# Two streams of the weights in place of three for experts with up to 64 tokens, chosen by a branch on TensorE

## The chip, the cores and the metric

The kernel runs on one core of a Trainium2 chip. The metric is the time of one execution on the device, in microseconds. A core has TensorE (PE in the profile; its weight loads are PEld), VectorE (DVE), ScalarE (ACT), GpSimd (POOL) and SyncE (SP), each with its own stream of instructions. They meet through semaphores. The DMA engines move data between HBM and the on-chip memory (SBUF); matmuls write into accumulator banks (PSUM).

## The reference

A decoder trunk of two layers over 256 tokens of width 1024, in float32. Each layer has an attention mixer and a feed-forward part; the second layer's feed-forward part is a mixture of eight experts, of which each token uses the two with the largest router logits:

```python
def swiglu(h, w_gate, w_up, w_down):
    return (jax.nn.silu(h @ w_gate) * (h @ w_up)) @ w_down
...
logits = (hf @ router_w).astype(jnp.float32)
top_logit, top_e = lax.top_k(logits, TOP_K)
gate = jax.nn.softmax(top_logit, axis=-1)
...
# every token goes through its two experts; their outputs, weighted by gate, are added
```

w_gate and w_up are 1024 x 3584 for each expert, w_down is 3584 x 1024: 44 MB of weights per expert, 352 MB in all, each read once.

## The kernel before

**Precision.** The matmuls take fp32r operands, which hold fewer bits than fp32. So every fp32 operand is split into an exact sum of two fp32r parts, hi and lo, and a product is three matmuls: x_hi w_hi, x_lo w_hi, x_hi w_lo (`product3`, L364, the matmuls L366 to L368). The weights stream through the three as the moving operand (128 x 512 columns); the tokens are the stationary operand of 128 x 128.

**Weights.** `Weights` (L53) has a list of pieces of 1 MB, 2048 columns on 128 partitions. `load` (L64) issues the DMA of a piece on SP's queue (L71) into a buffer named raw; for the experts there are 4 + 8 such buffers. `take` (L80) makes the two parts of a piece in two halves of 1024 columns: ACT copies raw to fp32r (whi, L94), DVE subtracts that from raw (wlo, L95). There are five buffers of each part (N_PART). A buffer pair is free again when the last matmul that reads it is done, and a raw buffer when both halves are split.

**Experts.** `moe` handles one expert after another. `gather` (L819) picks the expert's tokens into 128 slots (xe, two parts, by matmuls with a one-hot matrix `so`); a slot holds one token, unused slots are zero. An expert with more than 128 tokens is handled by `beyond`, behind a branch at the end (L974); no expert of this input has so many. The 3584 hidden columns are done in seven chunks of 512. For each chunk:

- gate: eg = x w_gate, 8 blocks of 128 rows, 24 matmuls; ACT makes esg = silu (L906);
- up: eu = x w_up, 24 matmuls; DVE makes ehc = eu * esg (L908);
- turn: four transposes of ehc (eT, L914); ACT and DVE split them into eth (L301) and etl (L302);
- down: ey += h w_down, 4 blocks by 2 column halves, 24 matmuls; the bank pair ey is kept over the seven chunks.

Each of the three takes two pieces of weights, four halves, so a chunk has 12 splits on ACT and 12 on DVE, and loads 6 MB.

**Order.** The program is written gate(n), turn(n-1), up(n), down(n-1) (`gate_up`, with `between`). The instructions are placed on each engine by a scheduler that knows which tiles each of them reads and writes, so turn and down may stand elsewhere. Behind an expert's last chunk come `weigh` (yhl, the outputs times their gates, split) and four `scatter` steps, which add the rows back to the tokens (acc, L890); `place` (L855) makes the matrix for it in the chunk with c == 1, and `gather` of the next expert stands at c == 3.

## Time and profile before

| | |
|---|---|
| median of three runs | 1553.09 us (1552.73 to 1553.78) |
| the profiled execution, from first to last instruction | 1555.6 us |
| PE busy | 1527.9 us, 98% |
| DVE busy | 1235.4 us, 79% |
| ACT busy | 1026.8 us, 66% |
| POOL busy | 7.8 us, 17 instructions |
| DMA | 436.94 MB, 281 GB/s over the span |
| mean granted clock of TensorE | 0.993 of full speed |

The profile's times run from the first to the last instruction of one execution; the runs are timed apart from it, with 2.5 us less at the median. "Busy" of PE counts a matmul from its start to its modelled end, and matmuls overlap, so PE is better read by the distance between starts. The part of the time that matters here is the experts' stage, from about 535 to 1548 us. Averages over the whole span mix it with attention and the dense layer.

### The profile page before, as it was taken

Reading aid. Unit: us, or ns where it says so; the run is one execution under the profiler, and the core shown is the slowest. Engines: PE = TensorE matmul, PEld = TensorE weight load, DVE = VectorE, ACT = ScalarE, POOL = GpSimd, SP = SyncE. Lnnn points to the kernel's source line nnn. Section 1 sums busy time; section 2 is a strip of 40 time slices with the busy share of each in tenths; the row PEclk is TensorE's granted clock in tenths of the full one; section 3 lists DMA queues with packets and bytes.
Section 4 is the critical chain, followed back from the end, with each engine's and each line's share of the span. In section 5 each row is a group of like instructions: output and inputs, shape, how many; then the busy total and the mean of one; then the engine's idle time right before and its main releaser. Section 6 shows DMA issues by size and latency. Waiting matters only on the chain.

```text
span 1555.6 us, 20636 instructions
## 1 busy us (share of the span) xinstructions
PE 1527.9 (98%) x7502; PEld 1234.2 (79%) x7502; DVE 1235.4 (79%) x1771; ACT 1026.8 (66%) x1389; POOL 7.8 (1%) x17
## 2 busy tenths in 40 slices
PE   7999999999999999999999999999999999999997
PEld 6767888888777888888888878887887887887885
DVE  5567755555766798998998888988888889888886
ACT  5445644445545587887787777767777776767774
POOL 2000000000000000000000000000000000000000
PEclk9999999999999999999999999999999999999999
DMA  8812455557626499999999989999999999999980
GB/s 263 292 55 82 157 178 177 200 189 234 229 96 217 167 357 331 379 357 329 361 363 333 363 320 336 344 356 342 326 370 352 327 358 346 329 352 365 353 323 29
DMA packets 200907, 436.94 MB, mean 281 GB/s; under 512 B 9448, under 2 KB 26080, under 8 KB 200800
## 3 DMA queue, kind: packets, MB, share of 16 engines
q1 hardware_dynamic: 198160, 434.63, 79.2%
q8 instruction: 61, 1.00, 0.3%
q10 hardware_dynamic: 2176, 0.52, 0.2%
q0 software_dynamic: 464, 0.40, 0.1%
q14 instruction: 46, 0.38, 0.1%
HBM read 433.92 MB, written 1.08 MB: 280 GB/s over the span
## 4 chain that ended last, share of the span: by engine, by line
PE 95%; DMA 2%; DVE 2%; ACT 1%; issue 1%; SPq 0%; ACTq 0%; DVEq 0%
PE eu L368 7%; PE eg L368 7%; PE eu L367 6%; PE eu L366 6%; PE eg L367 6%; PE eg L366 6%; PE ey L366 6%; PE ey L367 6%; PE ey L368 6%; PE pj L368 3%; PE pj L366 3%; PE pj L367 3%; PE y L368 2%; PE y L367 2%; PE y L366 2%; PE o L502 2%
## 5 line engine op out<-in xcount | busy, mean ns | idle before, releaser
L95 DVE TENSOR_TENSOR wlo<-raw,whi 128x1024 fp32r<-128x1024 f32 (+1 forms) x802 | 946.1, 1215 | 158.9 <-ACT whi L94 147.9
L94 ACT ACTIVATE whi<-raw 128x1024 fp32r<-128x1024 f32 (+1 forms) x802 | 807.0, 1051 | 188.7 <-PE y L367 45.2
L368 PE MATMUL eg<-wlo,xe 128*128 128x512 f32 x448 | 177.4, 396 | 1.5 <-DVE wlo L95 1.5
L368 PE MATMUL eu<-wlo,xe 128*128 128x512 f32 x448 | 178.6, 399 | 0.0
L366 PE MATMUL ey<-whi,eth 128*128 128x512 f32 x448 | 177.5, 397 | 0.7 <-ACT eth L301 0.7
L366 PE MATMUL eg<-whi,xe 128*128 128x512 f32 x448 | 176.8, 395 | 0.7 <-ACT xe L304 0.3
L366 PE MATMUL eu<-whi,xe 128*128 128x512 f32 x448 | 177.4, 396 | 0.0
L367 PE MATMUL ey<-whi,etl 128*128 128x512 f32 x448 | 176.8, 395 | 0.0
L367 PE MATMUL eg<-whi,xe 128*128 128x512 f32 x448 | 175.9, 393 | 0.0
L367 PE MATMUL eu<-whi,xe 128*128 128x512 f32 x448 | 175.2, 391 | 0.0
L368 PE MATMUL ey<-wlo,eth 128*128 128x512 f32 x448 | 165.7, 399 | 0.0
L368 PEld LDWEIGHTS eu<-wlo,xe 128*128 128x128 f32 x448 | 84.1, 188 | 23.9 <-DVE wlo L95 6.9
L368 PEld LDWEIGHTS eg<-wlo,xe 128*128 128x128 f32 x448 | 84.2, 188 | 22.4 <-DVE wlo L95 4.6
L366 PEld LDWEIGHTS ey<-whi,eth 128*128 128x128 f32 x448 | 84.3, 188 | 20.7 <-ACT eth L301 1.1
L367 PEld LDWEIGHTS ey<-whi,etl 128*128 128x128 f32 x448 | 84.5, 189 | 20.2 <-DVE etl L302 0.4
L366 PEld LDWEIGHTS eg<-whi,xe 128*128 128x128 f32 x448 | 84.2, 188 | 20.3 <-ACT whi L94 2.6
L367 PEld LDWEIGHTS eg<-whi,xe 128*128 128x128 f32 x448 | 84.1, 188 | 17.8
L367 PEld LDWEIGHTS eu<-whi,xe 128*128 128x128 f32 x448 | 84.2, 188 | 17.1
L366 PEld LDWEIGHTS eu<-whi,xe 128*128 128x128 f32 x448 | 84.2, 188 | 15.8
L368 PEld LDWEIGHTS ey<-wlo,eth 128*128 128x128 f32 x448 | 82.5, 188 | 17.4
L301 ACT ACTIVATE eth<-eT 128x512 fp32r<-128x512 f32 x56 | 33.1, 592 | 88.7 <-PE ey L368 75.0
L366 PE MATMUL pj<-whi,uhi 128*128 128x512 f32 (+1 forms) x192 | 76.3, 399 | 0.8 <-ACT qv L411 0.8
(299 smaller groups left out, 1970.5 us busy)
## 6 DMA issues: line engine op xcount, KB each, us to landing
raw<-in_exp_w_gate_dram SPq DMA_DIRECT2D x112, 1024.0 KB, 7.0
raw<-in_exp_w_up_dram SPq DMA_DIRECT2D x112, 1024.0 KB, 7.0
raw<-in_exp_w_down_dram SPq DMA_DIRECT2D x112, 1024.0 KB, 6.8
raw<-in_w_in_dram SPq DMA_DIRECT2D x20, 1024.0 KB, 6.0
raw<-in_ffn_w_gate_dram SPq DMA_DIRECT2D x10, 1024.0 KB, 5.1
raw<-in_ffn_w_up_dram SPq DMA_DIRECT2D x10, 1024.0 KB, 5.2
raw<-in_ffn_w_down_dram SPq DMA_DIRECT2D x10, 1024.0 KB, 5.1
raw<-in_cmp_w_dram SPq DMA_DIRECT2D x8, 1024.0 KB, 6.2
```

Of the source, the lines that this page charges most:

```text
L94: self.nc.scalar.activation(hi[:, :m * w], src, AF.Copy)
L95: self.nc.vector.tensor_tensor(out=lo[:, :m * w], in0=src, in1=hi[:, :m * w].bitcast(F32), op=ALU.subtract)
L301: act.activation(hi, src, AF.Copy)
L366: pe.matmul(dst, xh, wh, start=first, stop=False)
L367: pe.matmul(dst, xl, wh, start=False, stop=False)
L368: pe.matmul(dst, xh, wl, start=False, stop=last)
L502: pe.matmul(o[:, hd * HD:(hd + 1) * HD], pt[:, c:c + 128], vpj[:, j, vc:vc + HD], start=(j == 0), stop=(j == nj - 1))
```

## The change

The experts' product is made in one of two ways. The number of an expert's tokens is read into a register on PE (`pe.value_load`), and `by_number` puts the matmuls of up, turn and down each into an If with an Else; the condition is number > 64. With more than 64 tokens, the matmuls are those of before. With up to 64, the tokens stand twice in the 128 slots (`own`): slots 0 to 63 and again 64 to 127. `mixed` makes, on POOL, a stationary operand with the hi parts in columns 0 to 63 and the lo parts in columns 64 to 127 (xm for up, htm for down). Then two matmuls per block do the work of three: xm w_hi and xm w_lo, so 16 in up and 16 in down, and the sums of the two slots of a token are added later: in turn by a matrix of two identities (`both`) in place of the transpose, at the end by the scatter. Gate stays as it was. `halves`, `ahead` and `take_half` split the weights ahead of their use, one half at a time, in list order, since a split can't stand inside an arm of a branch.

The diff, cut to its core (the other changed lines are comments, blank lines, and lines moved from further down):

```diff
-    def take(self):
-        """The two parts of the next piece, for each of its blocks of 128 rows."""
+    def halves(self):
         while self.used in self.plain:
             self.used += 1
         raw = self.take_raw(self.used)
         _, nk, w = self.specs[self.used]
         self.used += 1
-        out = []
...
-            out += [(hi[:, i * w:(i + 1) * w], lo[:, i * w:(i + 1) * w]) for i in range(m)]
-        return out
+            yield [(hi[:, i * w:(i + 1) * w], lo[:, i * w:(i + 1) * w]) for i in range(m)]
+
+    def take(self):
+        return [x for half in self.halves() for x in half]
+
+    def ahead(self, n, loads):
+
+        while n:
+            if self.open is None:
+                if self.used >= len(self.specs):
+                    return
+                self.open = self.halves()
+            half = next(self.open, None)
+            if half is None:
+                self.open = None
+                self.load(self.used + loads)
+            else:
+                self.ready.append(half)
+                n -= 1
+
+    def take_half(self):
+        return self.ready.pop(0)
...
+        few = mpool.tile([128, NE], F32, name="few")
+        dve.tensor_scalar(out=few, in0=cb[:, 0:NE], scalar1=64.0, scalar2=None, op0=ALU.is_le)
+        number = mpool.tile([128, NE], I32, name="number")
+        dve.tensor_copy(number, cb[:, 0:NE])
...
+        again = mpool.tile([128, 128], F32, name="again")
+        dve.memset(again[:, 0:64], 0.0)
+        dve.memset(again[:, 64:128], -64.0)
+        both = mpool.tile([128, 128], F32, name="both")
+        for i in range(2):
+            dve.tensor_tensor(out=both[:, i * 64:(i + 1) * 64], in0=ident[:, 0:64], in1=ident[:, 64:128], op=ALU.add)
...
+            own = mpool.tile([128, 128], F32, name="own", tag="own")
+            dve.scalar_tensor_tensor(out=own, in0=again, scalar=few[:, e:e + 1], in1=slot, op0=ALU.mult, op1=ALU.add)
             so = mpool.tile([128, NT, 128], F32, name="so", tag="so", bufs=2)
             for t in range(NT):
-                dve.tensor_scalar(out=so[:, t, :], in0=slot, scalar1=pos[:, t, e:e + 1], scalar2=None,
+                dve.tensor_scalar(out=so[:, t, :], in0=own, scalar1=pos[:, t, e:e + 1], scalar2=None,
...
-            held[e] = so, x, rl
+            held[e] = so, x, rl, pe.value_load(number[0:1, e:e + 1], min_val=0, max_val=S)
...
-        def gate_up(e, c, between):
...
-            hc = mpool.tile([128, 512], F32, name="ehc", tag="ehc", bufs=2)
+        def by_number(e, many, few):
+
+            with tc.If(held[e][3] > 64) as cond:
+                many()
+            with cond.Else():
+                few()
+
+        def mixed(src, name, n):
+
+            dst = mpool.tile([128, n, 128], F32R, name=name)
+            pool.tensor_copy(dst.rearrange("p k (i t) -> p i k t", i=2), src[:, :, :, 0:64])
+            return dst
+
+        def gate(e):
+            _, x, rl, _ = held[e]
+            b = mm_bank("eg")
+            for half in range(4):
+                for k, (wh, wl) in enumerate(ws.take_half(), half * 2):
+                    product3(b, x[:, 0, k, :], x[:, 1, k, :], wh, wl, k == 0, k == KD - 1)
+                ws.ahead(1, deep)
+            sg = mpool.tile([128, 512], F32, name="esg", tag="esg")
+            act.activation(sg, b, AF.Silu, scale=rl)
+            return sg
+
+        def up(e, sg):
+            _, x, rl, _ = held[e]
+            b = mm_bank("eu")
+            xm = state["xm"]
+            w = [x for _ in range(4) for x in ws.take_half()]
+
+            def many():
+                for k, (wh, wl) in enumerate(w):
+                    product3(b, x[:, 0, k, :], x[:, 1, k, :], wh, wl, k == 0, k == KD - 1)
+
+            def few():
+                for k, (wh, wl) in enumerate(w):
+                    pe.matmul(b, xm[:, k, :], wh, start=(k == 0), stop=False)
+                    pe.matmul(b, xm[:, k, :], wl, start=False, stop=(k == KD - 1))
+
+            by_number(e, many, few)
+            hc = mpool.tile([128, 512], F32, name="ehc", tag="ehc")
             dve.scalar_tensor_tensor(out=hc, in0=b, scalar=rl, in1=sg, op0=ALU.mult, op1=ALU.mult)
             return hc
 
-        def turn(hc):
+        def turn(e, hc):
             b = tr_bank("eT")
-            for f in range(4):
-                pe.transpose(b[:, f * 128:(f + 1) * 128], hc[:, f * 128:(f + 1) * 128], ident)
-            th = mpool.tile([128, 4, 128], F32R, name="eth", tag="eth")
-            tl = mpool.tile([128, 4, 128], F32R, name="etl", tag="etl")
-            split_psum(th.rearrange("p f t -> p (f t)"), tl.rearrange("p f t -> p (f t)"), b)
-            return th, tl
-
-        def down(e, c, th, tl):
+
+            def many():
+                for f in range(4):
+                    pe.transpose(b[:, f * 128:(f + 1) * 128], hc[:, f * 128:(f + 1) * 128], ident)
+
+            def few():
+                for f in range(4):
+                    pe.matmul(b[:, f * 128:(f + 1) * 128], hc[:, f * 128:(f + 1) * 128], both, start=True, stop=True)
+
+            by_number(e, many, few)
+            ht = mpool.tile([128, 2, 4, 128], F32R, name="eth", tag="eth")
+            split_psum(ht[:, 0].rearrange("p f t -> p (f t)"), ht[:, 1].rearrange("p f t -> p (f t)"), b)
+            return ht, mixed(ht, "htm", 4)
+
+        def down(e, c, ht):
             if c == 0:
                 state["y"] = [acc_bank("ey") for _ in range(2)]
             y = state["y"]
             final = c == len(MOE_CHUNKS) - 1
-            w = []
-            for half in range(2):
-                w += ws.take()
-                ks = range(4) if half else ()
-                if not final:
-                    ks = range(half * 2, half * 2 + 2)
-                for k, n in [(k, n) for n in range(2) for k in ks] if final else [(k, n) for k in ks for n in range(2)]:
+            w = [x for _ in range(4) for x in ws.take_half()]
+            ht, htm = ht
+            steps = [(k, n) for n in range(2) for k in range(4)] if final else [(k, n) for k in range(4) for n in range(2)]
+
+            def many():
+                for k, n in steps:
                     f = slice(n * 512, (n + 1) * 512)
-                    product3(y[n], th[:, k, :], tl[:, k, :], w[k][0][:, f], w[k][1][:, f],
+                    product3(y[n], ht[:, 0, k, :], ht[:, 1, k, :], w[k][0][:, f], w[k][1][:, f],
                              c == 0 and k == 0, final and k == 3)
+
+            def few():
+                for k, n in steps:
+                    f = slice(n * 512, (n + 1) * 512)
+                    pe.matmul(y[n], htm[:, k, :], w[k][0][:, f], start=(c == 0 and k == 0), stop=False)
+                    pe.matmul(y[n], htm[:, k, :], w[k][1][:, f], start=False, stop=(final and k == 3))
+
+            by_number(e, many, few)
...
-        parts_of = []
-
-        def between():
-            if prev is not None:
-                parts_of[:] = turn(prev[2])
-
+        deep = N_RAW + SPARE
+        ws.ahead(N_PART, deep)
         for i, (e, c) in enumerate(seq):
             if c == 3 and e + 1 < NE:
                 gather(e + 1)
-            hc = gate_up(e, c, between)
+            if c == 0:
+                state["xm"] = mixed(held[e][1], "xm", KD)
+            sg = gate(e)
+            ht = None
             if prev is not None:
-                down(*prev[:2], *parts_of)
+                ht = turn(prev[0], prev[2])
+            hc = up(e, sg)
+            ws.ahead(4, deep)
+            if prev is not None:
+                down(*prev[:2], ht)
+                ws.ahead(4, deep)
             for _ in range(PER if c else 0):
                 if left:
                     scatter(*left.pop(0))
             prev = (e, c, hc)
-        between()
-        down(*prev[:2], *parts_of)
+        down(*prev[:2], turn(prev[0], prev[2]))
```

The change moves instructions on every engine. Names carry a number for each use of a buffer. On PE, in a chunk of a later expert, the stretch from the end of up to the turn stood like this before: eu is the up product of this chunk, ey are the two halves of the down product of the chunk ahead of it, ehc_10095 is what DVE makes from eu_10050.

```order
L367 MATMUL ey_9439<-whi_10099,etl_10045 128x512
L366 MATMUL ey_9440<-whi_10099,eth_10044 128x512
L367 MATMUL ey_9440<-whi_10099,etl_10045 128x512
L368 MATMUL ey_9439<-wlo_10100,eth_10044 128x512 [waits DVE_49]
L368 MATMUL ey_9440<-wlo_10100,eth_10044 128x512
L366 MATMUL ey_9439<-whi_10103,eth_10044 128x512 [waits Activation_49]
L367 MATMUL ey_9439<-whi_10103,etl_10045 128x512
L366 MATMUL ey_9440<-whi_10103,eth_10044 128x512
L367 MATMUL ey_9440<-whi_10103,etl_10045 128x512
L914 MATMUL eT_10186<-cc_70,ehc_10095 128x128 [waits DVE_49]
L914 MATMUL eT_10186<-cc_70,ehc_10095 128x128 x3
L368 MATMUL ey_9439<-wlo_10104,eth_10044 128x512 [waits DVE_49]
```

Ten matmuls of down stand there between the last of up and the turn; the row behind the turn goes on with down.

On PE after the change, from the last matmuls of up's second arm: eu_8880 is this chunk's up product, ehc_8922 is made from it, eg_9007 is the next chunk's gate product, L978 and L982 are the two arms of the turn, and ey_7928 begins down.

```order
L386 MATMUL eg_9007<-whi_8940,xe_8200 128x512 [waits Activation_49]
L931 COMPARE_AND_BRANCH
L978 MATMUL eT_9054<-cc_70,ehc_8922 128x128 [waits DVE_49,PE_49]
L978 MATMUL eT_9054<-cc_70,ehc_8922 128x128 x3
L931 UNCONDITIONAL_BRANCH
L982 MATMUL eT_9054<-both_4756,ehc_8922 128x128 [waits DVE_49,PE_49]
L982 MATMUL eT_9054<-both_4756,ehc_8922 128x128 x3
L931 UNCONDITIONAL_BRANCH
L387 MATMUL eg_9007<-whi_8940,xe_8200 128x512
L931 COMPARE_AND_BRANCH
L386 MATMUL ey_7928<-whi_8859,eth_8875 128x512
```

One gate matmul now stands between up and the turn, and one between the turn and down, which is now a block of its own.

On PE, the end of that down block (second arm) and what follows:

```order
L1008 MATMUL ey_7928<-wlo_8935,htm_8878 128x512 [waits DVE_49]
L1007 MATMUL ey_7929<-whi_8934,htm_8878 128x512
L1008 MATMUL ey_7929<-wlo_8935,htm_8878 128x512
L931 UNCONDITIONAL_BRANCH
L388 MATMUL eg_9007<-wlo_8941,xe_8200 128x512 [waits DVE_49]
L386 MATMUL eg_9007<-whi_8940,xe_8200 128x512
L387 MATMUL eg_9007<-whi_8940,xe_8200 128x512
L388 MATMUL eg_9007<-wlo_8941,xe_8200 128x512
L386 MATMUL eg_9007<-whi_8985,xe_8200 128x512 [waits Activation_49]
```

Gate goes on with its first buffer pair (whi_8940) only behind the whole down block.

On ACT before, the splits that stand beside up's end and down in the same chunk (whi_10099 to whi_10125 are down's four halves, whi_10144 and whi_10148 the next gate's):

```order
L94 ACTIVATE whi_10099<-raw_10097 128x1024 [waits DMAHW5_49,DVE_49]
L94 ACTIVATE whi_10103<-raw_10097 128x1024 [waits DVE_49,PE_49]
L94 ACTIVATE whi_10121<-raw_10119 128x1024 [waits DMAHW6_49,DVE_49,PE_49]
L94 ACTIVATE whi_10125<-raw_10119 128x1024 [waits DVE_49,PE_49]
L94 ACTIVATE whi_10144<-raw_10142 128x1024 [waits DMAHW7_49,DVE_49,PE_49]
L94 ACTIVATE whi_10148<-raw_10142 128x1024 [waits DVE_49,PE_49]
L301 ACTIVATE eth_10191<-eT_10186 128x512 [waits PE_49]
L94 ACTIVATE whi_10166<-raw_10164 128x1024 [waits DMAHW0_49,DVE_49]
```

They follow each other, and each waits for the matmuls that free its buffer pair, within up or down.

On ACT after (whi_8934 is down's last half, whi_8940, whi_8985, whi_8991 and whi_8995 the next gate's four, whi_9001 and whi_9014 the first two of the next up):

```order
L94 ACTIVATE whi_8934<-raw_8560 128x1024 [waits DVE_49,PE_49]
L94 ACTIVATE whi_8940<-raw_8611 128x1024 [waits DMAHW1_49,DVE_49,PE_49]
L931 UNCONDITIONAL_BRANCH x2
L94 ACTIVATE whi_8985<-raw_8611 128x1024 [waits DVE_49,PE_49]
L94 ACTIVATE whi_8991<-raw_8621 128x1024 [waits DMAHW2_49,DVE_49,PE_49]
L94 ACTIVATE whi_8995<-raw_8621 128x1024
L94 ACTIVATE whi_9001<-raw_8648 128x1024 [waits DMAHW3_49]
L94 ACTIVATE whi_9014<-raw_8648 128x1024 [waits DVE_49,PE_49]
```

whi_8985 waits for a count of PE within the down block, whi_8991 for one that the gate matmuls behind that block reach; the rows after it stand behind it in ACT's queue.

## Rows read from the trace of the kernel before

**Rows 1.** Page, part 4: the chain that ended last, by engine, by line.

```profile
PE 95%; DMA 2%; DVE 2%; ACT 1%; issue 1%; SPq 0%; ACTq 0%; DVEq 0%
PE eu L368 7%; PE eg L368 7%; PE eu L367 6%; PE eu L366 6%; PE eg L367 6%; PE eg L366 6%; PE ey L366 6%; PE ey L367 6%; PE ey L368 6%; PE pj L368 3%; PE pj L366 3%; PE pj L367 3%; PE y L368 2%; PE y L367 2%; PE y L366 2%; PE o L502 2%
```

**Rows 2.** Windows: start:end, length, busy of PE, PEld, DVE, ACT, POOL, clock, DMA share, GB/s.

```profile
600.00:1500.00 900.00, 898.03 (x4113) 730.00 (x4112) 806.70 (x811) 673.62 (x769) 0.00 (x0) 1.00 0.97 349
640.00:660.00 20.00, 20.00 (x93) 16.43 (x92) 18.38 (x18) 16.12 (x18) 0.00 (x0) 1.00 1.03 387
```

**Rows 3.** Chain of waits in pieces, four places: start, us, what.

```profile
918.03 4.80 DMA raw<-in_exp_w_down_dram
...
1008.79 0.23 PE eu L367
...
1011.58 0.44 PE eT L914 x4
...
1045.40 4.76 DMA raw<-in_exp_w_down_dram
```

**Rows 4.** Timeline of SP's queue, two loads of gate weights: start, us, engine, line.

```profile
1380.76 3.91 SPq L71 DMA_DIRECT2D raw<-in_exp_w_gate_dram  x2
...
1397.86 3.91 SPq L71 DMA_DIRECT2D raw<-in_exp_w_gate_dram  x2
```

**Rows 5.** Waits of SP's queue, 840 to 1540 us: total us, times, longest.

```profile
SPq L71 <- DVE wlo L95: 552.4, 216, 5.3
```

**Rows 6.** Lines, 840 to 1540 us, shapes apart: busy us, mean ns, idle before.

```profile
L95 DVE TENSOR_TENSOR wlo<-raw,whi 128x1024 fp32r<-128x1024 f32 x465 | 542.8, 1219 | 37.0 <-ACT whi L94 34.9
L94 ACT ACTIVATE whi<-raw 128x1024 fp32r<-128x1024 f32 x465 | 455.6, 1052 | 12.5 <-PE ey L367 6.0 <-PE eg L367 4.4 <-PE eu L367 1.7
...
L908 DVE SCALAR_TENSOR_TENSOR ehc<-eu,rl,esg 128x512 f32<-128x512 f32 x39 | 29.3, 750 | 18.0 <-PE eu L368 18.0
L302 DVE TENSOR_TENSOR etl<-eT,eth 128x512 fp32r<-128x512 f32 x40 | 27.5, 688 | 10.3 <-ACT eth L301 10.3
...
L890 DVE TENSOR_TENSOR acc<-acc,scat 128x512 f32<-128x512 f32 x22 | 15.0, 683 | 3.1 <-PE scat L889 3.1
...
L305 DVE SCALAR_TENSOR_TENSOR xe<-ga,gv,xe 128x128 fp32r<-128x128 f32 x34 | 10.7, 344 | 1.0 <-ACT xe L304 1.0
...
L305 DVE SCALAR_TENSOR_TENSOR yhl<-ey,gs,yhl 128x512 fp32r<-128x512 f32 x10 | 7.0, 746 | 5.0 <-ACT yhl L304 5.0
```

**Rows 7.** Timeline, all engines, 1002 to 1013 us: start, us, what.

```profile
1008.40 0.39 PE L366 MATMUL eu<-whi,xe 128*128 128x512 f32 x1
...
1008.62 0.39 PE L367 MATMUL eu<-whi,xe 128*128 128x512 f32 x1
...
1009.95 3.48 DVE L95 TENSOR_TENSOR wlo<-raw,whi 128x1024 fp32r<-128x1024 f32 x3
```

**Rows 8.** Windows, early in the program, columns as in rows 2.

```profile
48.76:52.17 3.41, 1.72 (x10) 0.97 (x9) 3.41 (x18) 0.53 (x1) 0.00 (x0) 1.00 1.10 348
52.17:55.58 3.41, 3.41 (x35) 2.09 (x33) 3.27 (x15) 0.00 (x0) 0.00 (x0) 0.50 0.73 193
```

**Rows 9.** Timeline of PE in the second of these: start, us, what.

```profile
52.31 0.63 PE L368 MATMUL pj<-wlo,uhi 128*128 128x512 f32 x1
52.74 0.63 PE L366 MATMUL pj<-whi,uhi 128*128 128x512 f32 x1
```

**Rows 10.** Line L974, the branch before the program's end, by engine: duration in ns.

```profile
L974 ACTq COMPARE_BRANCH  x1: 54/54/54, 1545.6 to 1545.6; - x1
...
L974 PEldq COMPARE_BRANCH  x1: 4622/4622/4622, 1548.2 to 1548.2; - x1
L974 DVEq COMPARE_BRANCH  x1: 72/72/72, 1549.0 to 1549.0; - x1
```

**Rows 11.** Page, part 3: the queue of instructions: packets, MB, share.

```profile
q8 instruction: 61, 1.00, 0.3%
```

More of the change, by code (lines that the diff above doesn't have):

```diff
@@ L816, in moe @@
                                  op0=ALU.add, op1=ALU.mult)
+        cb = tr_bank("count")
+        for t in range(NT):
+            pe.matmul(cb[:, 0:NE], ones, sel[:, t, :], start=(t == 0), stop=(t == NT - 1))
+        few = mpool.tile([128, NE], F32, name="few")
+        dve.tensor_scalar(out=few, in0=cb[:, 0:NE], scalar1=64.0, scalar2=None, op0=ALU.is_le)
+        number = mpool.tile([128, NE], I32, name="number")
+        dve.tensor_copy(number, cb[:, 0:NE])
+        most = mpool.tile([128, 1], F32, name="most")
+        dve.tensor_reduce(out=most, in_=cb[:, 0:NE], axis=AX.X, op=ALU.max)
+        again = mpool.tile([128, 128], F32, name="again")
[4 more added lines that the diff above has]
+            dve.tensor_tensor(out=both[:, i * 64:(i + 1) * 64], in0=ident[:, 0:64], in1=ident[:, 64:128], op=ALU.add)
         rs = row_rstd(h, D, "h")
         def gather(e):
+            own = mpool.tile([128, 128], F32, name="own", tag="own")
+            dve.scalar_tensor_tensor(out=own, in0=again, scalar=few[:, e:e + 1], in1=slot, op0=ALU.mult, op1=ALU.add)
             so = mpool.tile([128, NT, 128], F32, name="so", tag="so", bufs=2)
             for t in range(NT):
-                dve.tensor_scalar(out=so[:, t, :], in0=slot, scalar1=pos[:, t, e:e + 1], scalar2=None,
+                dve.tensor_scalar(out=so[:, t, :], in0=own, scalar1=pos[:, t, e:e + 1], scalar2=None,
                                   op0=ALU.is_equal)
@@ L867, in place @@
             return st, gs
-        cb = tr_bank("count")
-        for t in range(NT):
-            pe.matmul(cb[:, 0:NE], ones, sel[:, t, :], start=(t == 0), stop=(t == NT - 1))
-        most = mpool.tile([128, 1], F32, name="most")
-        dve.tensor_reduce(out=most, in_=cb[:, 0:NE], axis=AX.X, op=ALU.max)
         flag = mpool.tile([128, 1], I32, name="flag")
@@ L893, in moe @@
         state = {}
-        def gate_up(e, c, between):
-            _, x, rl = held[e]
-            for w in range(2):
-                b = mm_bank("eg" if w == 0 else "eu")
-                for half in range(2):
-                    for k, (wh, wl) in enumerate(ws.take(), half * 4):
-                        product3(b, x[:, 0, k, :], x[:, 1, k, :], wh, wl, k == 0, k == KD - 1)
-                    if (w, half) == (0, 1):
-                        between()
-                if w == 0:
-                    sg = mpool.tile([128, 512], F32, name="esg", tag="esg")
-                    act.activation(sg, b, AF.Silu, scale=rl)
-            hc = mpool.tile([128, 512], F32, name="ehc", tag="ehc", bufs=2)
+        def by_number(e, many, few):
[3 more added lines that the diff above has]
+                few()
```

5 lines of the change are left out of this document (2 added, 3 removed).

## Prediction

> **What bounds the kernel now.** I read the chain of waits first. TensorE (PE) makes 95% of it and the DMA queues 2%, in hundreds of matmuls of three lines [rows 1]. The page has no row for the experts, so I took stretches. From 600 to 1500 us PE is busy 898.03 of 900.00 us at clock 1.00, VectorE (DVE) 806.70, ScalarE (ACT) 673.62, and the DMA engines have a share of 0.97 at 349 GB/s [rows 2]. So PE sets the end there, but DMA and DVE follow within 3 and 10%: whatever PE gives up, at most a few per cent can come out. One expert lasts 127.37 us (1045.40 − 918.03, the same load one expert later, [rows 3]); a plain chunk of its seven lasts 17.10 us (1397.86 − 1380.76, [rows 4]). The queue of loads waits for DVE's split of the weights, 552.4 us over 216 waits [rows 5]: the splits free the buffers that are loaded into. Per chunk DVE has twelve splits, and these [rows 6] are the longest work outside PE.
>
> **Which experts take the new way.** The reference, run with its inputs, routes 63, 57, 40, 75, 39, 90, 68 and 80 tokens to the eight experts. Four of them take two streams, four keep three; 28 chunks each.
>
> **What is removed.** A matmul step is 0.23 us [rows 3]. Up goes from 24 to 16 matmuls, down too: 16 × 0.23 = 3.68 us per chunk of a small expert, 28 × 3.68 = 103 us of PE time in all. Gate stays at 24. This is the ceiling, and the DMA rate cuts it: six loads of 1.05 MB per chunk at the highest rate seen, 387 GB/s in 640 to 660 us [rows 2], take 16.3 us, so a chunk can't fall from 17.1 below that, 28 × 0.8 = 22 us.
>
> **What is moved: the loop.** Two moves matter more than the matmuls. First, before, the turn of a chunk's product stands behind 10 matmuls of the down block, which cover DVE's making of ehc; after, one gate matmul stands between up and turn. Second, before, ACT's splits go on all through down, because each group of down's matmuls frees a buffer pair. After, of the splits queued during down, the first (whi_8985 in the order shown) waits for a matmul inside the down block, and the next (whi_8991) for a count that is reached only by a gate matmul on whi_8940 that stands behind the whole block. With five buffer pairs, all later splits on ACT and with them on DVE queue behind it. That closes a loop through three engines. From that gate matmul on:
> ACT's split 1.05 us, then DVE in a row nine wlo, the second half of eth and ehc. A wlo takes 3.48/3 = 1.16 us undisturbed [rows 7]; the others 0.69 and 0.75 [rows 6]. So 1.05 + 10.44 + 0.69 + 0.75 = 12.93 us until ehc is there. PE: turn 0.44 [rows 3], one gate matmul 0.23, down 3.68 (16) or 5.52 (24), three gate matmuls 0.69. Hand-overs between engines I put at 0.4 (a matmul lasts 0.39 [rows 7] and its successor starts after 0.23, so the last one of a block costs 0.16 more; two more crossings at about 0.1). Sum: 18.4 us small, 20.2 us large, against 17.1: +1.3 and +3.1. The gate and up matmuls, which lose the most, are not in the loop: gate ends 5 us after the release, a small up at 9.3, when its last wlo is there, and PE then stands idle until 13.0, about 3.7 us (some 2.6 where up has 24). The saving of up falls into this idle time; that of down is in the loop.
> Chunks that carry more: the one that closes an expert has a tenth wlo, two yhl at 0.75 and one acc at 0.68 in the row (21.7 and 23.5 us); the one with the placing and a scatter 20.0 and 21.8; the one that gathers 8 xe at 0.34 has no such wait, and DVE's row sets 19.5 and 21.5. Four standard chunks, these three and 0.7 for the other acc: 4 × 18.4 + 21.7 + 20.0 + 19.5 + 0.7 = 135.5 per small expert, 4 × 20.2 + 23.5 + 21.8 + 21.5 + 0.7 = 148.3 per large one, against 127.4. Over the eight: 4 × 8.1 + 4 × 20.9 = +116 us.
>
> **What is added.**
> *The clock.* PE in this stage never rests before. After, it rests 3.7 us in each small chunk. Early in the trace there is such a place: PE busy 1.72 of 3.41 us at clock 1.00, and in the 3.41 us after it the clock is 0.50, that is 1.2 GHz, with matmul steps of 0.43 us (52.74 − 52.31) [rows 8, 9]. A lowered stretch like that costs at most 3.41/2 = 1.7 us, and follows the idle time, so it lies mostly on turn and down, which are in the loop. I take 1.5 us per small chunk and 0.9 per large one, where the rest is shorter: 28 × 1.5 + 28 × 0.9 = +67 us; bounds 0 (the rests don't lower it) and 56 × 1.7 = 95.
> *The copies on GpSimd (POOL)*, one htm per chunk, one xm per expert. No copy on POOL stands in the trace of before. Its own time is hidden, since htm is used a chunk later. What it does to DVE is unknown: from nothing (or a little less, since ACT and DVE keep their work as it is) to one wlo of 1.15 us held up per chunk, 64 us. The nearest row is etl of the same size, 0.69 us [rows 6], part of which falls in DVE's gaps; I take 0.5, so +28.
> The Trainium skill ("SBUF — State Buffer", Who interferes with whom) says that a DVE instruction with two SBUF inputs, as wlo is, contends with a GpSimd instruction that reads SBUF, and that the later one waits in full. By it the sum would be nearer the upper end, some +36 on mine; no run here shows it yet, and my value stands on the rows.
> *The branches.* Three pairs of arms per chunk; each engine runs through a branch instruction there. Those at the program's end show 54 ns on ACT and 72 on DVE [rows 10]. On the loop lie one of DVE and four of PE: 0.3 us per chunk, 56 × 0.3 = +17; bounds 3 (hidden but for DVE's own) and 60. The one row of PE, 4.62 us, lies at the end of the program and is a rival below.
> *Small things.* The count is made earlier, with two identities added, before the first expert: a few DVE instructions under a microsecond, hidden beside the loads or not, within the branches' bounds. One register load per expert on PE waits for nothing that is late.
>
> **Sum.** 1555.6 + 116 + 67 + 28 + 17 = 1784 us against the profiled execution's own span; the median of the runs, 1553.09, is 2.5 below that span, so I forecast 1781. With the bounds of clock, copies and branches it reaches from 1672 (all at the low end) to 1855 (95 + 64 + 27); nine wlo at their mean 1.22 us [rows 6] in place of 1.16 add another 30 at most.
>
> **Rivals.**
> 1. *The loop alone* (chance 0.17): the rests don't lower the clock and POOL disturbs nothing. For it: PE is at 1.00 over the whole stage, and a rest of 2 to 4 us in 18 is a small share. Against: the row from 48.76 us, with a rest of much the same kind, and the clock behind it [rows 8]. 1672 to 1715, about 1690.
> 2. *Instruction fetch* (0.11): a jump of PE that leaves what is loaded costs what the branch at the end cost, 4.62 us [rows 10]. Queue 8 brought 61 packets with 1.00 MB of instructions, 16.4 KB each [rows 11]. If these are PE's 15,004, one is 67 bytes, and an arm of 24 matmuls (48 instructions) 3.2 KB, so about one skipped arm in five, some 1 chunk in 3, crosses a packet's end: 20 × 4.6 = 92 us on the loop, about 1873. Against: matmuls queued ahead may hide it, and the arms lie in sequence.
> The Trainium skill ("Runtime: NRT & Kernel Launch", Instruction fetch mechanics) states such a fetch for a taken branch whose target is not in the loaded pages, in blocks of 16 KiB. The packet size in the trace agrees; the price of a jump inside the program no run here shows.
> 3. *Faster* (0.06): the splits are not held up by the down block, because enough of them stand ahead of it. Then DVE bounds a small expert: 7 chunks × (12 × 1.16 + 0.75 + 0.69) = 107.5, plus 8 xe 2.8, two yhl 1.5 and four acc 2.7, 114.5 us; the loads need 7 × 16.3 = 114. 4 × (127.4 − 114.5) = 52 us gained, less 17 for the branches: about 1518. For it: DVE has 3 us of rest in the loop's 18.4, and the order is tight by one buffer pair. It decides where a release comes one group of down earlier. Against: the order of ACT's waits as it is built.
> 4. *No change* (0.03): the loop's loss in the large experts (some 3 us a chunk) is less, because up and turn overlap better than I assume, and the small ones gain as much: 1550 to 1556.
> 5. *The small arm is never taken* (0.03): all eight at 20.9 above, 167 us, with 50 for the clock and 45 for copies and branches: about 1815.
>
> **How the numbers follow.** My forecast has 0.60, with its own range 1715 to 1850. Rivals 1, 2 and 5 are slower too: slower by over 0.2% has 0.60 + 0.17 + 0.11 + 0.03 = 0.91. 0.2%, 3 us, is about what a measurement of this kernel can tell from no change. Faster has 0.06, the same 0.03. The range from 1665 to 1860 leaves out rivals 3 and 4 and most of rival 2, with a little of my forecast's tails: 0.2.
>
> **What would show it.** Small chunks of about 18.4 to 20 us and large ones of about 20 to 22 us between two gate loads. On PE a rest before each turn, put down to DVE's ehc. On DVE nine wlo without a gap ahead of ehc, and then a rest on ACT's whi, which itself waits for a gate matmul. The granted clock below 1.00 in most chunks; were it 1.00, rival 1 is right. PE branches of microseconds mean rival 2. wlo longer than 1.22 us beside POOL's copies show their price. Small chunks below 17 us would make the loop wrong, and the whole forecast with it.

## The result and the profile after

The changed kernel takes 1732.84 us (median of four runs, 1729.38 to 1733.63), the kernel before 1553.43 beside it (1552.73 to 1555.72): a ratio of 1.1145 (95% interval 1.1129 to 1.116). The forecast was 1781, so the sign and the range held and the sum was some 50 us too high. The profiled execution spans 1730.3 us, 174.7 more than before; the medians are 179.4 apart, since the profiled execution of the kernel before is 2.5 us longer than its median and that of the kernel after 2.5 us shorter.

The chain of waits of the kernel after, by engine, answers to [rows 1]: PE has fallen from 95% of it to 68, and DVE and ACT, 3% together before, have 21.

```profile
PE 68%; DVE 16%; DMA 6%; ACT 5%; issue 4%; SPq 0%; POOL 0%; DVEq 0%; ACTq 0%; POOLq 0%
```

A window over most of the experts' stage of the kernel after, columns as in [rows 2]. PE was busy in 99.8% of its window before and is in 86% now (947.39 of 1100), VectorE falls from 90 to 75%, the DMA share from 0.97 to 0.82: no engine is full, so they wait for each other in turn.

```profile
600.00:1700.00 1100.00, 947.39 (x3957) 728.12 (x3958) 828.40 (x843) 678.67 (x794) 102.78 (x59) 0.94 0.82 291
```

Whom they wait for: the waits of the kernel after, 840 to 1700 us (engine, line, releaser; total us, times, longest us). In the stretch of [rows 6] ACT's splits idled 6.0 us on `ey` and 4.4 on `eg`. Now two short lists of long waits, for a gate matmul (L387, eg) and for a down matmul (L387, ey), hold 187 us, and DVE's half of the split waits for ACT's.

```profile
DVE wlo L95 <- ACT whi L94: 118.7, 42, 7.9
ACT whi L94 <- PE eg L387: 104.6, 27, 10.2
ACT whi L94 <- PE ey L387: 82.1, 19, 6.8
```

One turn of the loop in a small expert's chunk, by engine, from timelines of the kernel after (start, us, engine, line, work, idle before). ACT and DVE first:

```profile
921.50 6.75 ACT L94 ACTIVATE whi<-raw 128x1024 fp32r<-128x1024 f32 x7 [3.11 <-PE eg L387]
...
922.59 8.04 DVE L95 TENSOR_TENSOR wlo<-raw,whi 128x1024 fp32r<-128x1024 f32 x7 [2.95 <-ACT whi L94]
930.54 0.68 DVE L322 TENSOR_TENSOR eth<-eT,eth 128x512 fp32r<-128x512 f32 x1
931.15 2.35 DVE L95 TENSOR_TENSOR wlo<-raw,whi 128x1024 fp32r<-128x1024 f32 x2
933.41 0.74 DVE L970 SCALAR_TENSOR_TENSOR ehc<-eu,rl,esg 128x512 f32<-128x512 f32 x1
```

And PE, over the turn before it and this one:

```profile
914.12 1.47 PE L982 MATMUL eT<-both,ehc 128*128 128x128 f32 x8 [0.57 <-DVE ehc L970]
...
920.37 0.39 PE L1008 MATMUL ey<-wlo,htm 128*128 128x512 f32 x1
...
921.07 0.40 PE L387 MATMUL eg<-whi,xe 128*128 128x512 f32 x1
...
930.13 0.39 PE L966 MATMUL eu<-wlo,xm 128*128 128x512 f32 x1
933.14 0.50 PE L386 MATMUL eg<-whi,xe 128*128 128x512 f32 x1 [2.62 <-ACT whi L94]
934.31 0.91 PE L982 MATMUL eT<-both,ehc 128*128 128x128 f32 x6 [0.67 <-DVE ehc L970]
```

The gate matmul at 921.07 ends the block behind down; ACT's split starts at 921.50 on it. From 922.59 VectorE has no gap: nine wlo, the second half of eth, ehc, ready at 934.15, 12.65 us after the release. Up has ended at 930.13 and PE stands until 933.14. Turn to turn (914.12 to 934.31) it is 20.19 us.

Windows of the same place in the kernel after, columns as in [rows 2]: the rest, then the turn and the first half of down. The clock is 1.00 in the rest, 0.58 on average in the 4 us behind it and 1.00 again from 918.4 on (the steps of down's matmuls fall back from 0.43 to 0.23 us).

```profile
911.00:914.00 3.00, 0.50 (x1) 0.19 (x1) 3.00 (x5) 1.99 (x3) 2.61 (x1) 1.00 0.97 354
914.20:918.20 4.00, 4.00 (x15) 3.42 (x16) 2.13 (x2) 0.87 (x1) 0.00 (x0) 0.58 1.08 393
```

SP's queue of the kernel after, loads of gate weights, columns as in [rows 4]. The first two are one small expert apart (902.58 − 755.71 = 146.87 us), the third and last one large (150.83), against 127.37 before [rows 3]; between the other two lies a large standard chunk, 19.90.

```profile
755.71 2.67 SPq L72 DMA_DIRECT2D raw<-in_exp_w_gate_dram  x2
...
902.58 2.67 SPq L72 DMA_DIRECT2D raw<-in_exp_w_gate_dram  x2
...
1350.90 2.69 SPq L72 DMA_DIRECT2D raw<-in_exp_w_gate_dram  x2
...
1389.75 5.17 SPq L72 DMA_DIRECT2D raw<-in_exp_w_gate_dram  x2
1409.65 5.18 SPq L72 DMA_DIRECT2D raw<-in_exp_w_gate_dram  x2
...
1501.73 2.67 SPq L72 DMA_DIRECT2D raw<-in_exp_w_gate_dram  x2
```

Taken for all eight, four experts at 19.5 more and four at 23.5 more make 172 of the 174.7 us.

### The profile page after: what moved, and what is told of

Its sections match the earlier page's. It is cut to its first block, busy times and chain, and to the rows that moved or that the text cites. A ratio compares the mean times of both kernels' runs of the same rounds, so it can differ in the third digit from the quotient of the medians.

```text
span 1730.3 us, 20316 instructions
## 1 busy us (share of the span) xinstructions
PE 1538.4 (89%) x7166; PEld 1199.2 (69%) x7166; DVE 1227.2 (71%) x1785; ACT 1005.9 (58%) x1389; POOL 122.2 (7%) x81
## 3 DMA queue, kind: packets, MB, share of 16 engines
q8 instruction: 80, 1.31, 0.3%
## 4 chain that ended last, share of the span: by engine, by line
PE 68%; DVE 16%; DMA 6%; ACT 5%; issue 4%; SPq 0%; POOL 0%; DVEq 0%; ACTq 0%; POOLq 0%
DVE wlo L95 12%; ACT whi L94 5%; DMA raw<-in_exp_w_up_dram 5%; PE ey L1007 4%; PE ey L1008 4%; PE ey L386 3%; PE ey L387 3%; PE eg L387 3%; PE eg L388 3%; PE ey L388 3%; PE pj L388 3%; PE pj L386 2%; PE pj L387 2%; PE eg L386 2%; PE eT L982 2%
## 5 line engine op out<-in xcount | busy, mean ns | idle before, releaser
L387 PE MATMUL eg<-whi,xe 128*128 128x512 f32 x448 | 186.7, 417 | 0.2 <-DVE xe L325 0.2
L939 POOL CAST htm<-eth 128x512 fp32r<-128x512 f32 x56 | 105.6, 1886 | 1059.8 <-DVE eth L322 1040.0
L1007 PE MATMUL ey<-whi,htm 128*128 128x512 f32 x224 | 103.2, 461 | 0.0
L1008 PE MATMUL ey<-wlo,htm 128*128 128x512 f32 x224 | 101.1, 451 | 0.0
L387 PEld LDWEIGHTS eg<-whi,xe 128*128 128x128 f32 x448 | 87.4, 195 | 16.4 <-DVE xe L325 0.6
L966 PE MATMUL eu<-wlo,xm 128*128 128x512 f32 x224 | 94.2, 421 | 0.6 <-DVE wlo L95 0.2
L387 PE MATMUL ey<-whi,eth 128*128 128x512 f32 x224 | 93.0, 415 | 1.1 <-DVE eth L322 1.1
L388 PE MATMUL ey<-wlo,eth 128*128 128x512 f32 x224 | 92.0, 411 | 0.0
L965 PE MATMUL eu<-whi,xm 128*128 128x512 f32 x224 | 90.0, 402 | 1.3 <-POOL xm L939 1.3
L388 PE MATMUL eu<-wlo,xe 128*128 128x512 f32 x224 | 87.6, 391 | 0.0
L387 PE MATMUL eu<-whi,xe 128*128 128x512 f32 x224 | 87.2, 389 | 0.0
L386 PE MATMUL eu<-whi,xe 128*128 128x512 f32 x224 | 87.2, 389 | 0.0
L388 PE MATMUL pj<-wlo,uhi 128*128 128x512 f32 (+1 forms) x192 | 75.1, 392 | 0.8 <-DVE wlo L95 0.8
L387 PE MATMUL pj<-whi,ulo 128*128 128x512 f32 (+1 forms) x192 | 74.7, 389 | 0.0
```

The costliest lines, as they stand in the source:

```text
L386: pe.matmul(dst, xh, wh, start=first, stop=False)
L387: pe.matmul(dst, xl, wh, start=False, stop=False)
L388: pe.matmul(dst, xh, wl, start=False, stop=last)
L939: pool.tensor_copy(dst.rearrange("p k (i t) -> p i k t", i=2), src[:, :, :, 0:64])
L965: pe.matmul(b, xm[:, k, :], wh, start=(k == 0), stop=False)
L966: pe.matmul(b, xm[:, k, :], wl, start=False, stop=(k == KD - 1))
```

## The experiments

Times are medians; the kernel before beside them took between 1552.61 and 1553.17 us.

**ring.** Buffer pairs are handed to splits in strict turn, and the experts' splits keep their written order. The computation and the branches stay. No run separates the two halves of this edit.

```diff
-            hi = self.part_pool.tile([128, 1024], F32R, name="whi", tag="whi", bufs=self.n_part)
+            slot = self.turns % self.n_part
+            self.turns += 1
+            hi = self.part_pool.tile([128, 1024], F32R, name="whi", tag=f"whi{slot}")
...
+                self.pin(one)
+                self.pin(two)
...
+        ws.pin = tc.keep_in_program_order
```

> The changed kernel with the buffer pairs used in strict turn and the experts' splits kept in written order, so that each split that stands behind the down block waits only for its own group of down's matmuls. Turn and branches as in the changed kernel. Loop theory: DVE goes on through down; a small chunk falls to about 16.5 us (the loads' 16.3), a large one to about 18.9 (72 x 0.23 = 16.6, turn and the uncovered ehc 2.3): 4 x (7 x 16.5 + 8) + 4 x (7 x 18.9 + 8) = 1055 us against 1019 before, so about 1590 (1565 to 1615). Rival, the branches' own price: within 20 us of 1733. Rival, GpSimd's copies: the same.

Measured: 1563.27, ratio 1.0068 (1.0048 to 1.0088), a little below the range expected. Some 170 of the 179 us are gone, with every other part of the change still there; the mean clock is back from 0.955 to 0.993, so what the clock had cost is among the 170. Timelines of ACT and DVE in this kernel, one small chunk, show what was predicted of rival 3: splits go on while down runs, DVE has one gap of 0.18 us in twelve wlo, eth and ehc, and turn to turn it is 15.16 us.

```profile
744.77 4.85 ACT L97 ACTIVATE whi<-raw 128x1024 fp32r<-128x1024 f32 x5 [1.52 <-PE ey L1013]
...
741.91 13.71 DVE L98 TENSOR_TENSOR wlo<-raw,whi 128x1024 fp32r<-128x1024 f32 x12
755.53 0.68 DVE L328 TENSOR_TENSOR eth<-eT,eth 128x512 fp32r<-128x512 f32 x1
756.40 0.75 DVE L976 SCALAR_TENSOR_TENSOR ehc<-eu,rl,esg 128x512 f32<-128x512 f32 x1 [0.18 <-PE eu L972]
```

A small expert falls to 119.4 us (701.07 to 820.45 in the loads of SP's queue), but a large one stands at 136.2 (1202.00 to 1338.17), since PE still rests 0.9 us before each turn, which no longer stands inside down.

**noif.** No branch at all: `many()` is called always, three streams for every expert. (In this kernel, and in ring_three and ring_order_three below, the tokens of a small expert count twice.)

```diff
-            with tc.If(held[e][3] > 64) as cond:
-                many()
-            with cond.Else():
-                few()
+            many()
```

> The changed kernel without any branch: always three streams, splits taken ahead one half at a time, the matmuls free to be ordered by the scheduler, which puts the turn into down again, 10 matmuls behind up. If the loss comes from the blocks that the branches make (splits behind down, turn behind up): 1553 to 1562. If splitting ahead itself costs: above 1600.

Measured: 1558.53, ratio 1.0034 (1.0019 to 1.0049), as expected. The loss is not in the new numbering of tokens nor in POOL's copies, which are all still made here, but in the blocks that the branches make. ACT's waits in this kernel, 600 to 1500 us: the wait for down is now 62 times short.

```profile
ACT whi L94 <- PE ey L387: 19.9, 62, 0.5
```

**late** and **ring_late.** PE's order as it is written (gate, turn, up, down), alone and with ring's edit, so that up covers the making of eth.

```diff
+        with tc.manual_schedule(engines={mybir.EngineType.PE}):
```

> The changed kernel with PE's instructions in written order: the whole gate, turn, up, down. The turn then has 24 gate matmuls between it and up. Splits and branches as in the changed kernel. Loop theory: ehc is off the loop; what is left of it (splits, gate, up, down) takes about 16 us in a small chunk and PE's own 17.6 in a large one: about 1555 (1540 to 1585). If only the splits' wait behind down counts and not the place of the turn: 1690 to 1730. Branch price or GpSimd copies: within 20 us of 1733.

> Both edits together. Loop theory: the small chunks are bound by loads and DVE at 16.3 to 16.5 us, the large ones by PE at 72 x 0.23 + 0.5 + 0.5 = 17.6, against 17.1 before: 1553 - 28 x 0.7 + 28 x 0.5 = 1547 (1530 to 1565). Branch price or GpSimd copies: above 1650.

Measured: late 1660.29, ratio 1.0688 (1.067 to 1.0707), ring_late 1594.37, 1.0271 (1.0248 to 1.0294); both missed. The order alone does not take the splits out from behind down, and turn and down now stand close enough that down waits for POOL's htm. Waits of late, 840 to 1500 us:

```profile
ACT whi L94 <- PE eg L387: 129.4, 48, 6.7
...
PE ey L1007 <- POOL htm L939: 32.2, 12, 3.5
```

In both, the chunk that gathers the next expert's tokens takes 24 to 30 us, as PE stands in line behind DVE's xe. Here a fixed order on one engine alone turned late neighbours into waits.

**busy.** Matmuls that nobody reads behind up (14 in the small arm, 9 in the large), to keep PE's rests filled and its clock up.

```diff
+                rest(9)
...
+                rest(14)
```

> The changed kernel with 14 extra matmuls (small arm) or 9 (large arm) behind up, into a bank that nobody reads, on operands that are there: they fill 3.2 and 2.1 us of PE's rest ahead of the turn. Clock as one term of the loss: the granted clock stays at 1.00, a small chunk falls from 20.2 to about 18.7 us, every fourth large one from 21.5 to 19.9, in all 28 x 1.5 + 7 x 1.6 = 53 us: about 1680 (1665 to 1700). If the clock's loss lies only where PE waits anyway: 1725 to 1740. If the clock were the whole loss: about 1560.

Measured: 1718.47, ratio 1.1068 (1.1046 to 1.109), 14 us less than after, where 53 were expected. The mean clock rose from 0.955 to 0.988, but the scheduler also moved the turn behind down, where PE waits for POOL. So the price of the clock isn't isolated by a run; below it is read from two loops of one trace.

```profile
806.95 0.50 PE L1016 MATMUL ey<-whi,htm 128*128 128x512 f32 x1 [1.46 <-POOL htm L939]
```

**ring_swap** and **ring_three.** ring, with the turn held behind the down block; ring_three has a condition besides that is always true, so all experts take three streams (the last two lines). Its trace holds no branch of PE in the experts' stage (252 in ring_swap), and its instructions came in 61 packets, as in [rows 11], against 80 in ring_swap: the second arms and the branches are not in the program that ran.

```diff
+                tc.add_manual_dep(head, state["down"].name,
+                                  mybir.DependencyInfo(mybir.DependencyClass.NoSync, mybir.DependencyReason.DATA),
+                                  reason="turn behind down")
...
-            with tc.If(held[e][3] > 64) as cond:
+            with tc.If(held[e][3] > -1) as cond:
```

> The changed kernel with the splits as in the run ring (buffer pairs in strict turn, splits in written order), and on PE the turn held behind the down block that was written ahead of it: up, two gate matmuls, down, turn, rest of gate. In the run ring a large chunk took 17.98 us, of which PE stood still 0.93 between up and the turn for ehc; here down covers that. Loop theory: large chunks about 17.2 us, small ones stay at 15.2 (DVE's twelve wlo and two more). Small experts 119, large ones 131 against 127.4: 1563 - 28 x 0.8 = about 1540 (1530 to 1555). If the rest is the jumps' and not ehc's, nothing changes: 1558 to 1568.

> As ring_swap, but the condition is always true, so that every expert takes three streams: branches, copies and order are there, nothing is saved. It prices the construct. By the large chunks above, 8 x (131 - 127.4) = +29: about 1583 (1570 to 1600). If branches cost microseconds: above 1640. If they cost nothing: 1553 to 1560.

Measured: 1623.32, ratio 1.0451 (1.0437 to 1.0465), and 1660.97, 1.0698 (1.0679 to 1.0718); both missed. Two gate matmuls had come to stand between up and down, and their buffer is freed only by up's last matmul: PE's timeline in ring_swap shows the rest at each block. So ring_three does not price the branches, as was meant; but its standard chunks of three streams take 18.17 us between turns with no branch in them, those of ring_swap 18.17 with them.

```profile
1318.60 0.39 PE L394 MATMUL eu<-wlo,xe 128*128 128x512 f32 x1
1320.03 0.50 PE L392 MATMUL eg<-whi,xe 128*128 128x512 f32 x1 [1.04 <-ACT whi L97]
```

**nopool.** No htm copy on POOL; down of a small expert reads the high part alone.

```diff
-            return ht, mixed(ht, "htm", 4)
+            return ht, ht[:, 0]
```

> The changed kernel without POOL's copy of htm: down's small arm reads the hi part alone (the lo part of the small experts' products is left out). Instructions of the other engines as they are. If the copy holds up DVE as I priced it, 0.5 us a chunk: about 1705. If DVE, coming first, makes the copy wait (it lasts 2.61 us there, 0.61 elsewhere) and nothing waits for it: 1726 to 1737.

Measured: 1729.26, ratio 1.1138 (1.1117 to 1.1159): 3.6 us less than after, where 28 were predicted for the copies. The intervals of the two ratios overlap, so even the 3.6 are not clear of the noise. This is the second of the two outcomes expected.

**ring_order** and **ring_order_three.** ring, with PE's order held at up, down, turn, gate, and two of down's splits ahead of ehc; the second again with three streams for all.

```diff
+                    if k == 0:
+                        behind(one.ins, state.get("down"), "gate behind down")
...
+            ws.ahead(2, deep)
```

> The splits as in the run ring; on PE the next gate and the turn both held behind the down block (up, down, turn, gate), and two of down's splits put ahead of ehc on DVE. In ring_swap two gate matmuls stood between up and down and waited for a split whose buffer only up's last matmuls free: PE stood still 0.9 us there in a large chunk (eg at 1320.03 behind eu at 1318.60) and 2.7 in a small one. Loop theory: nothing on PE then waits for a buffer that is freed just before it: large chunks 72 x 0.23 + 0.5 + 0.3 = 17.3 us, small ones 15.2 by DVE: 1530 to 1550. If the jumps or the turn's second arm cost what is lost: 1560 to 1625.

> As ring_order, with a condition that is always true: every expert takes three streams (the small experts' tokens stand twice, so their outputs are counted twice). Prices branches, jumps and copies with nothing saved: 56 chunks of 17.3 against 17.1: 1565 (1555 to 1580). If a jump costs a microsecond: above 1640.

Measured: 1564.9, ratio 1.0087 (1.0069 to 1.0105), and 1576.97, 1.0156 (1.0137 to 1.0175); the first missed. The second lies in its range, but, like ring_three, it ran with no branch of PE in the experts' stage (61 packets of instructions), so it is ring_order's order without the branches. That makes the pair a test of their price. PE's branches in ring_order, and in ring_order_three SP's loads of gate weights, one standard chunk apart:

```profile
L938 PEldq COMPARE_BRANCH  x252: 65/175/350, 539.0 to 1543.6; - x126
```

```profile
1282.33 2.64 SPq L73 DMA_DIRECT2D raw<-in_exp_w_gate_dram  x2
1299.20 2.64 SPq L73 DMA_DIRECT2D raw<-in_exp_w_gate_dram  x2
```

A standard chunk of three streams takes 16.87 us with the branches (1283.38 − 1266.51 in SP's queue of ring_order) and 16.87 without, both below the 17.10 of [rows 4]: where PE sets the pace, the branches cost nothing that can be seen. Small chunks of ring_order take between 14.85 and 16.5, as PE waits for htm (its waits, 840 to 1500 us):

```profile
PEld ey L1023 <- POOL htm L952: 18.6, 9, 3.9
```

**act_copy** and **scat_late.** As ring_order, with ACT making htm behind its first split (the first line); then, besides, the scatter written between turn and up in place of behind down, its addition on DVE behind the splits ahead of it.

```diff
+                tc.keep_in_program_order(act.activation(to, frm, AF.Copy))
...
+            for _ in range(PER if c else 0):
+                if left:
+                    scatter(*left.pop(0))
```

> As ring_order, with ACT in place of POOL making htm, behind the first of the splits that up frees. In ring_order the large chunks came to 16.87 us (17.1 before), but the small ones alternate between 14.9 and 16.5 and PE waits 33.6 us for POOL's htm from 840 to 1500 us, a copy that stands still while DVE subtracts. Theory: with the copy on ACT a small chunk is bound by DVE's own 15.1 to 15.4 us; small experts 119 to 121, large ones 129.5 as there: 4 x -7.4 + 4 x 2.1 = -21, and 8 at the stage's start and end as in the run ring: about 1540 (1528 to 1552). Rival: the copy on ACT holds up the splits behind it, and the small chunks stay near 16.5: 1558 to 1570.

> As act_copy, with the scatter written between turn and up, and its addition on DVE held behind the splits written ahead of it. In act_copy DVE waits 31.6 us for scatter matmuls from 840 to 1500 us, some 6 us per expert, with splits queued behind: the additions stood ahead of gate's splits, the matmuls behind the turn. Theory: DVE's queue bounds the small experts, and half of that wait comes back: 8 x 3 = 25 us, about 1530 (1518 to 1545). Rival: DVE's wait lies beside waits for loads or PE: 1548 to 1556.

Measured: act_copy 1553.3, ratio 1.0006 (0.9991 to 1.002), a miss by little: DVE, which bounds the small experts, waited 31.6 us for the scatter's matmuls from 840 to 1500 us, nearly as long as in ring_order (32.1). scat_late 1513.74, ratio 0.9742 (0.9727 to 0.9757): faster than both kernels, and by more than was expected of it. A window of scat_late over three small chunks, columns as in [rows 2], and from its SP queue the loads that begin and end one small and one large expert:

```profile
717.00:764.00 47.00, 44.13 (x197) 34.14 (x196) 45.97 (x45) 41.12 (x46) 1.68 (x1) 1.00 1.03 386
```

```profile
700.04 3.16 SPq L73 DMA_DIRECT2D raw<-in_exp_w_gate_dram  x2
...
816.93 3.15 SPq L73 DMA_DIRECT2D raw<-in_exp_w_gate_dram  x2
...
1156.75 2.64 SPq L73 DMA_DIRECT2D raw<-in_exp_w_gate_dram  x2
...
1282.47 2.64 SPq L73 DMA_DIRECT2D raw<-in_exp_w_gate_dram  x2
```

A small expert takes 116.9 us, 10.5 less than before, a large one 125.7, 1.7 less. In the small chunks DVE is busy 98% of the time and the DMA engines move 386 GB/s, about the highest rate of [rows 2], so the window doesn't tell which of the two bounds them. What scat_late's order would do for three streams alone was not run; the large experts, which take three, gained 1.7 us each, some 14 us if all eight did.

## Why the prediction was right, and where it was not

| us | predicted | measured |
|---|---|---|
| small standard chunk, loop at full clock | 18.4 | 18.55 (see below) |
| its clock loss | 1.5 | 1.59 |
| large standard chunk | 20.2, + 1.7 for clock, copies, branches | 19.9, every fourth 21.5 |
| POOL's copies, whole program | 28 | about 4, within the noise |
| small expert, all terms | 151.6 | 146.9 |
| large expert, all terms | 160.2 | 150.8 |

*The loop* was right in mechanism and close in size. Each turn of it begins with a release, where ACT's split starts on the gate matmul behind down: 921.50 in the rows above, then 941.64 and 960.19. Windows over the two loops between these releases, columns as in [rows 2], and the two ACT rows:

```profile
921.50:941.64 20.14, 16.49 (x65) 12.23 (x64) 15.06 (x14) 12.64 (x14) 2.61 (x1) 0.92 0.89 316
941.64:960.19 18.55, 14.88 (x65) 11.09 (x64) 15.80 (x14) 12.65 (x15) 3.59 (x2) 1.00 0.91 319
```

```profile
941.64 6.75 ACT L94 ACTIVATE whi<-raw 128x1024 fp32r<-128x1024 f32 x7 [3.39 <-PE eg L387]
...
960.19 6.75 ACT L94 ACTIVATE whi<-raw 128x1024 fp32r<-128x1024 f32 x7 [2.59 <-PE eg L387]
```

Both hold the same work: twelve wlo, the second half of eth and ehc on DVE, 24 gate matmuls, 16 of up, 16 of down and the turn on PE. The second ran at clock 1.00 throughout: 18.55 us, against 18.4 predicted. Until ehc it is 12.65 us (12.93 predicted).

That the waits behind down are the loss is shown: ring takes them away and 170 us go, noif takes the blocks away and 174 go. Why a split stands behind the block is read from the order in the program and the two runs agree with it: an If with its arms is one piece for the scheduler, so the free buffer pairs come from behind it, and strict turn gives back those of its middle.

*That up's saving falls into idle time* was right. In a small and in a large chunk ehc comes equally late, 12.65 and 12.67 us after the release; PE's rest ahead of the turn is 3.3 us in the small one (2.62 and 0.67 in the rows above) and 1.9 in the large one, whose up is 8 matmuls longer. 3.7 and 2.6 were predicted. PE in a large chunk of the kernel after:

```profile
1402.71 0.50 PE L386 MATMUL eg<-whi,xe 128*128 128x512 f32 x1 [1.23 <-ACT whi L94]
1403.88 0.63 PE L978 MATMUL eT<-cc,ehc 128*128 128x128 f32 x4 [0.67 <-DVE ehc L970]
```

*The clock* was right for the small chunks: the first of the two loops above, with its clock lowered to 0.92 on average, took 20.14 us, 1.59 more than the second. It is read from two loops of one trace, and busy did not isolate it. For large chunks it was too high: three of four show 19.9, the loop's own length, and 1.6 more stands in the fourth, 0.4 a chunk in place of 0.9. Their rest is shorter, and the clock did not fall behind each of them.

*The copies* are the step that failed: "0.5 per chunk" held up on DVE. nopool, without htm, is 3.6 us shorter, and that within the noise. POOL waits instead. Timelines of POOL and DVE in the kernel after: the htm cast that falls beside back-to-back wlo takes 2.61 us, one beside an addition 0.61, and the wlo beside the long casts are undisturbed; where POOL started first (xm, once per expert) a wlo took 1.95 seven times, and 13 more took 1.30 or 1.31, each beside a short htm.

```profile
701.11 0.61 POOL L939 CAST htm<-eth 128x512 fp32r<-128x512 f32 x1 [19.98 <-DVE eth L322]
...
804.67 2.61 POOL L939 CAST htm<-eth 128x512 fp32r<-128x512 f32 x1 [17.55 <-DVE eth L322]
807.22 1.04 POOL L939 CAST xm<-xe 128x1024 fp32r<-128x1024 f32 x1
```

```profile
700.89 0.68 DVE L924 TENSOR_TENSOR acc<-h,scat 128x512 f32<-128x512 f32 x1
...
805.58 1.22 DVE L95 TENSOR_TENSOR wlo<-raw,whi 128x1024 fp32r<-128x1024 f32 x1
...
807.38 1.95 DVE L95 TENSOR_TENSOR wlo<-raw,whi 128x1024 fp32r<-128x1024 f32 x1
```

The Trainium skill ("SBUF — State Buffer", Who interferes with whom) says that issue order decides which of the two is blocked. The rows agree for the instruction that was first (1.95 against 1.22 on DVE behind xm, 2.61 against 0.61 on POOL behind a wlo), but not for the one after it: the cast stood from 804.67 to 807.28, while a second wlo began at 805.58 and took its 1.22. The prediction charged DVE with most of each copy, as if POOL were first. In 35 of 56 it was POOL that stood; that this is so because DVE had no gap is likely, but was not tested.

*The branches* at 0.3 a chunk were too dear if anything: those of PE take 65 to 355 ns, median 176 (252 of them in the kernel after), and a chunk that PE bounds takes 16.87 us with them and without (ring_order and ring_order_three). ring_order_three is 24 us over the kernel before though its experts' stage has no branch; its standard chunks are not longer, so these lie in the chunks that gather, close and scatter, and are not the branches'.

*Missed*: the turn's small arm issues eight passes, not four (below), about 0.45 us more on the loop in each of 28 chunks. By the spans the sum came out too high by 53 us. An estimate of where: POOL (some 24), the large chunks' clock (some 14, 28 × 0.5), the branches (up to 17) and the fuller chunks, less some 13 that the turn's small arm adds; branches and fuller chunks the runs do not separate here. Two slips of its sums changed nothing that counts: the upper bound of 1855 takes 27 us for the branches where the text gives 60, which would make 1888; and the 2.5 us from span to time did not hold for the kernel after, whose median lies above its span.

*Rivals.* Rival 1 is refuted in its first half, no clock loss, by the window at 0.58; its second, that POOL disturbs nothing, came nearly true; rival 2 by the branch durations, none of microseconds, and by the equal chunks with and without branches; rival 4 by the time; rival 5 by the small arm's rows. Rival 3's condition, a release inside down, is what ring made: 15.16 us per small standard chunk against its 12 × 1.16 + 0.75 + 0.69 = 15.36. It put DVE's 114.5 us on a small expert, and scat_late reached 116.9. The prediction's floor of 16.3 us for a chunk, from the DMA rate, was wrong for a single chunk (15.16 in ring), since loads run ahead; over seven (114 us) it held in the two runs with the fastest small experts shown (119.4 in ring, 116.9 in scat_late).

## What to carry to other kernels

A branch on one engine that encloses a block of matmuls did not cost its jump here; it took from the scheduler the releases inside the block and the work that it would have put there. Before putting a block under a branch, list whose buffers it frees on the way and what stands between its matmuls; hand such buffers out in strict turn, and write by hand the order that hid the small products. Where the engine that sheds work is followed within ten per cent by another (DVE here, and the DMA within three), the gain is at most what those leave; here it came only when the waits on DVE were taken away too: 1733, 1563, 1565, 1553, 1514 us. And a run that is to price a construct must still hold it: here a condition that is always true left no branch in the program.

## What the runs showed of the hardware

- A float32 matmul that does what a transpose did takes twice the passes: the profile counts eight for the four of L982 against four for the transposes. In ring, at clock 1.00, eight lasted 1.13 us and two 0.46, so 0.11 each and 0.9 for the turn, against 0.44 [rows 3].
- A POOL cast can be held over two DVE subtractions in a row, also over one that began after it: 0.61 us became 2.61 or more, in 35 of 56 casts, while those subtractions kept their 1.22.
- PE's 252 branch instructions at arms of up to 24 matmuls lasted 0.07 to 0.36 us each, while the branch at the program's end took 4.62 [rows 10]. Chunks bound by PE were as long with them as without: 16.87 us.
- The same loop, with the same rest of PE ahead of its turn (2.6 and 0.7 us), ran once at a mean clock of 0.92 and once at 1.00: 20.14 and 18.55 us.
